# Squared-ReLU MLP of a two-layer encoder trunk: one stream of weight chunks with a fixed order on every engine, and seven instead of five of sixteen row-tile pairs in Strassen's form

## The chip, the cores and the metric

The kernel runs on one NeuronCore of a Trainium2 chip, as one launch. The metric is the device time of one execution in microseconds; lower is better. Inputs and output are float32.

## The reference

The trunk has two layers on a sequence of S = 256 tokens with D = 2048 features. Layer 0 mixes tokens with a convolution module, layer 1 with latent attention; each is followed by the same kind of MLP, with an RMS norm ahead of every part and one at the end.

```python
D_MODEL = 2048; SEQ = 256; DEPTH = 2; D_FF = 4 * D_MODEL

def sq_relu_mlp(h, w1, w2):
    return jnp.square(jax.nn.relu(h @ w1)) @ w2

for layer in range(DEPTH):
    h = rms_norm(x, norm_mixer_g[layer])
    x = x + (conv_module(h, ...) if layer % 2 == 0 else mla(h, ...))
    h = rms_norm(x, norm_mlp_g[layer])
    x = x + sq_relu_mlp(h, mlp_w1[layer], mlp_w2[layer])
return rms_norm(x, final_norm_g)
```

w1 is 2048 x 8192 and w2 is 8192 x 2048 in each layer.

## The kernel before

Every float32 factor is split into a high part (`hi`, rounded to the format of the fast matmul, written by ScalarE, L159 and L389) and the rest (`lo`, a subtraction on VectorE, L160 and L390), and a product is three matmuls: hi with hi, lo with hi, hi with lo (`mm3`, L185 to L187). So each weight is loaded once (1 MB units, three `raw` buffers, issued by SyncE, L149), split once in chunks of 128 x 1024 (six buffers, `WB`), and used by both row tiles of 128 tokens.

The MLP goes through the 8192 hidden features in two halves (`HALVES`). In each half, `up` computes the hidden features in eight groups of four blocks of 128: 16 steps over D, each with a 512-column matmul (L514, the weight's hi part against hi and lo of the input side by side) and a 256-column one (L515) for every block. Two blocks make one pair p of the sixteen (`NPAIR`); its square is taken (L521 to L537) and split (L543, L544). Then `down` goes through the 2048 output columns in two column pairs `n2` of 2 x 512, and for each through the sixteen pairs p. A pair p is a product of a 2 x 2 block matrix (two row tiles by two feature blocks) with another (two feature blocks by two column blocks). A plain pair takes 8 block products, 24 matmuls. Where `seven(p)` holds (p = 0, 3, 6, 9, 12), it takes Strassen's form in Winograd's variant: 7 block products, 21 matmuls. Sums of activation blocks are made in `up` on VectorE and GpSimd (tile W, L525 to L533); sums of weight blocks, four tiles T, in `down` on VectorE (L449, L453, L455), and are then split (L389, L390).

The seven products gather in seven of the eight PSUM banks over all pairs of a column pair; the plain pairs add into three of them and the eighth. Behind the last Strassen pair (p = 12) `early` combines four of the banks (copies L431 and L432 on ScalarE, subtractions L433 and L434 on VectorE, L437 and L438 on GpSimd) and adds them to the residual `xs` (`xs_add`, L555); behind the last pair the other four are added. In the second half `prepare` then transposes blocks of `xs` into the next stage's input (L241, L191, L198) and takes the squares for the next norm (L340). In the last column pair of the last layer the three plain pairs behind p = 12 are kept back and computed output block by output block, so that the final norm (`before` with the gain at L1479, then `finish`) can follow block by block.

The order of the MLP's instructions on each engine is chosen by the scheduler of the programming layer from its own estimate of times. The convolution and the attention are written inside `manual_schedule()`, which keeps the written order on each engine within the block and leaves to the scheduler where the block's instructions fall among those outside it. Attention starts with `u_split` of its first weights (L160 with 128 x 576 tiles).

Of the kernel before, what the change touches and what calls it, by code (L numbers as in the profile page):

```python
# [10 lines left out]
F32 = mybir.dt.float32  # L11
# [7 lines left out]
P = 128  # L19
D = 2048  # L20
# [30 lines left out]
FILL_AT = (5, 15)  # L51
N_WARM = 14
# [24 lines left out]
def trunk_kernel(  # L77
# [306 lines left out]
    def split_part(src, eng):  # L384

        _, nj, cols = src.shape
        hi = wpool.tile([P, nj, cols], F32R, tag="hi", name=nm("hi"), bufs=WB)
        lo = wpool.tile([P, nj, cols], F32R, tag="lo", name=nm("lo"), bufs=WB)
        nc.scalar.activation(hi, src, AF.Copy)  # L389
        eng.tensor_tensor(lo, src, hi.bitcast(F32), op=ALU.subtract)  # L390
        return hi, lo
# [14 lines left out]
    def down(w, k_lo, hs, xs_add, prepare, pre, mp, finish=None, before=None):  # L406

        for n2 in range(NNB // 2):
            na, nb = 2 * n2, 2 * n2 + 1
            banks, seen = {}, set()  # L410
            outs = {(1, nb): "P2", (1, na): "Q3", (0, nb): "P4", (0, na): "Q0"}

# [6 lines left out]
            def plain(p, parts, n, t):  # L419
                for k in range(2):  # L420
                    wh, wl = parts[k]
                    gh, gl = (a[:, k, t * P : (t + 1) * P] for a in hs[p])
                    bs = slice((n - na) * NB, (n - na + 1) * NB)
                    mm(outs[t, n], gh, gl, wh[:, 0, bs], wl[:, 0, bs], p == NPAIR - 1 and k == 1)

            def early():

                s1, s5 = (mp.tile([P, NB], F32, tag="v", name=nm("v"), bufs=2) for _ in range(2))
                uv = mp.tile([P, 2, NB], F32, tag="W", name=nm("W"), bufs=1)
                u, v = uv[:, 0, :], uv[:, 1, :]  # L430
                nc.scalar.activation(s1, banks["P1"], AF.Copy)  # L431
                nc.scalar.activation(s5, banks["Q5"], AF.Copy)  # L432
                nc.vector.tensor_tensor(u, s1, banks["Q6"], op=ALU.subtract)  # L433
                nc.vector.tensor_tensor(v, u, banks["Q7"], op=ALU.subtract)  # L434
                xs_add(nb, s1, 1)
                xs_add(nb, v, 0)
                nc.gpsimd.tensor_tensor(u, s5, u, op=ALU.subtract)  # L437
                nc.gpsimd.tensor_tensor(v, s5, v, op=ALU.subtract)  # L438
                xs_add(na, u, 1)
                xs_add(na, v, 0)  # L440

            last = finish is not None and n2 == NNB // 2 - 1
            kept = []
            for p in range(NPAIR):
                raw = load([rows(w, k_lo + 2 * p, 2, na * NB, 2 * NB)], 2)
                if seven(p):
                    x = raw.rearrange("p j (b n) -> p (j b) n", b=2)
                    tt = mp.tile([P, 4, NB], F32, tag="T", name=nm("T"), bufs=1)
                    nc.vector.tensor_tensor(  # L449
                        tt[:, 0:2, :], x[:, 0:1, :].broadcast_to([P, 2, NB]), x[:, 1:3, :], op=ALU.add  # L450
                    )
                    one = split_part(x[:, 1:2, :], nc.vector)
                    nc.vector.tensor_tensor(tt[:, 2, :], tt[:, 0, :], x[:, 2, :], op=ALU.add)  # L453
                    t13 = split_part(tt[:, 0:2, :], nc.vector)
                    nc.vector.tensor_tensor(tt[:, 3, :], tt[:, 2, :], x[:, 3, :], op=ALU.add)  # L455
                    t24 = split_part(tt[:, 2:4, :], nc.vector)
# [1090 lines left out]
```

## Time and profile before

| | us |
|---|---|
| median of 3 runs | 1974.42 (1972.78 to 1976.09) |
| the profiled execution, its own time | 1974.39 |
| its span, first to last instruction | 1972.6 |
| TensorE busy in it | 1945.4 |
| VectorE, ScalarE, GpSimd busy | 1410.4, 1032.7, 311.0 |

The granted TensorE clock is 0.998 over the span. A line of the profile such as L187 is a line of the kernel above. PE is TensorE, DVE VectorE, ACT ScalarE, POOL GpSimd, SP SyncE. TensorE works through the first MLP's `up` and `down` from 316 to 1008 us, and through the second MLP's from 1269 us to the end.

### The profile page before, as it was taken

The page shows a single profiled execution, that of the slowest core. Times are in us where ns is not written, and L with a number is a line of the kernel's source. Part 1 is how long each engine was busy: PE and PEld are TensorE (multiplying, and loading weights), DVE is VectorE, ACT ScalarE, POOL GpSimd, SP SyncE. Part 2 cuts the span into 40 slices and gives each one's busy share as a digit, 9 for nine tenths or more (in the row PEclk, how much of TensorE's full clock was granted, in tenths as well). Part 3 has the DMA queues.
Part 4 walks back from the last instruction along what each step waited for, and adds up shares of the span by engine and source line. Part 5 has one row for each costly group of instructions (what it writes and reads, how often), then busy time and mean ns, then how long its engine had stood idle before and what let it go on. Part 6 is the DMA issues. An engine that isn't in the chain of part 4 may idle for free.

```text
span 1972.6 us, 28263 instructions
## 1 busy us (share of the span) xinstructions
PE 1945.4 (99%) x10940; PEld 1708.3 (87%) x10940; DVE 1410.4 (71%) x2043; ACT 1032.7 (52%) x1481; POOL 311.0 (16%) x260
## 2 busy tenths in 40 slices
PE   7999999999999999999999999999999999999997
PEld 7999888888888888888899998888888888888886
DVE  5999866666787766678776666566677776667786
ACT  5456655444544444455466665544454444445453
POOL 5999300010000101000001310010100001010000
PEclk9999999999999999999999999999999999999999
DMA  8666456655656665565655445566556676565563
GB/s 241 179 185 186 135 192 186 188 188 168 204 198 203 220 188 188 168 206 195 207 168 179 121 150 178 183 187 188 189 178 200 200 226 188 187 189 199 198 203 117
DMA packets 210502, 367.60 MB, mean 186 GB/s; under 512 B 15416, under 2 KB 89792, under 8 KB 210112
## 3 DMA queue, kind: packets, MB, share of 16 engines
q1 hardware_dynamic: 209344, 363.63, 58.1%
q10 hardware_dynamic: 1024, 2.17, 0.3%
q8 instruction: 85, 1.39, 0.3%
q14 instruction: 49, 0.40, 0.1%
HBM read 363.68 MB, written 2.10 MB: 185 GB/s over the span
## 4 chain that ended last, share of the span: by engine, by line
PE 89%; DVE 8%; ACT 1%; DMA 1%; issue 0%; POOL 0%; POOLq 0%; DVEq 0%; ACTq 0%
PE acc L514 24%; PE acc L187 15%; PE acc L186 15%; PE acc L185 15%; PE acc L515 12%; DVE sum L721 6%; PE acc L620 1%; PE acc L621 1%; PE acc L619 1%; PE acc L241 1%; DVE lo L160 1%; PE sum L669 0%; ACT hi L159 0%; PE acc L1317 0%; DMA xs<-in_x 0%
## 5 line engine op out<-in xcount | busy, mean ns | idle before, releaser
L160 DVE TENSOR_TENSOR lo<-raw,hi 128x1024 fp32r<-128x1024 f32 (+1 forms) x550 | 651.4, 1207 | 367.7 <-ACT hi L159 360.9
L159 ACT ACTIVATE hi<-raw 128x1024 fp32r<-128x1024 f32 (+2 forms) x616 | 622.5, 1040 | 432.4 <-PE acc L514 227.4
L514 PE MATMUL acc<-xt,hi 128*128 128x512 f32 x2048 | 710.5, 390 | 0.0
L515 PE MATMUL acc<-xt,lo 128*128 128x256 f32 x2048 | 578.4, 282 | 0.0
L514 PEld LDWEIGHTS acc<-xt,hi 128*128 128x128 f32 x2048 | 384.4, 188 | 79.7
L515 PEld LDWEIGHTS acc<-xt,lo 128*128 128x128 f32 x2048 | 388.0, 189 | 0.1
L187 PE MATMUL acc<-lo,gh 128*128 128x512 f32 x704 | 274.9, 391 | 2.0 <-DVE lo L160 2.0
L185 PE MATMUL acc<-hi,gh 128*128 128x512 f32 x704 | 274.8, 390 | 0.0
L186 PE MATMUL acc<-hi,gl 128*128 128x512 f32 x704 | 274.7, 390 | 0.0
L389 ACT ACTIVATE hi<-T 128x1024 fp32r<-128x1024 f32 x80 | 84.9, 1062 | 161.9 <-DVE T L449 72.6
L721 DVE SCALAR_TENSOR_TENSOR sum<-ub,w_dw,sum 128x256 f32<-128x256 f32 x400 | 163.7, 503 | 7.1 <-ACT sum L677 6.0
L160 POOL TENSOR_TENSOR lo<-raw,hi 128x1024 fp32r<-128x1024 f32 x66 | 157.5, 2407 | 23.9 <-ACT hi L159 23.9
L529 POOL TENSOR_TENSOR W<-W 128x256 f32<-128x256 f32 x20 | 31.9, 1598 | 819.9 <-DVE W L525 693.9
L185 PE MATMUL acc<-hi,sh 128*128 128x512 f32 x408 | 159.6, 391 | 0.0
L187 PE MATMUL acc<-lo,sh 128*128 128x512 f32 x408 | 159.0, 390 | 0.0
L187 PEld LDWEIGHTS acc<-lo,gh 128*128 128x128 f32 x704 | 132.8, 189 | 30.0 <-DVE lo L160 2.5
L186 PEld LDWEIGHTS acc<-hi,gl 128*128 128x128 f32 x704 | 132.5, 188 | 27.7
L185 PEld LDWEIGHTS acc<-hi,gh 128*128 128x128 f32 x704 | 132.5, 188 | 27.2
L619 PE MATMUL acc<-xt,hi 128*128 128x256 f32 x512 | 144.6, 282 | 0.0
L620 PE MATMUL acc<-xt,hi 128*128 128x256 f32 x512 | 143.2, 280 | 0.5 <-DVE xt L198 0.5
L621 PE MATMUL acc<-xt,lo 128*128 128x256 f32 x512 | 143.2, 280 | 0.3 <-POOL lo L160 0.3
L390 DVE TENSOR_TENSOR lo<-T,hi 128x1024 fp32r<-128x1024 f32 x80 | 97.9, 1225 | 51.6 <-ACT hi L389 51.3
(264 smaller groups left out, 2655.3 us busy)
## 6 DMA issues: line engine op xcount, KB each, us to landing
raw<-in_mlp_w SPq DMA_DIRECT2D x256, 1024.0 KB, 5.5
raw<-in_conv_w_pw SPq DMA_DIRECT2D x64, 512.0 KB, 5.1
raw<-in_conv_w_pw SPq DMA_DIRECT2D x16, 1024.0 KB, 5.0
raw<-in_mla_w_o SPq DMA_DIRECT2D x16, 1024.0 KB, 5.5
raw<-in_mla_w_kv_up SPq DMA_DIRECT2D x8, 1024.0 KB, 5.5
raw<-in_mla_w_in SPq DMA_DIRECT2D x8, 576.0 KB, 3.7
raw<-in_mla_w_in SPq DMA_DIRECT2D x4, 1024.0 KB, 7.1
raw<-in_mla_w_q_up SPq DMA_DIRECT2D x16, 256.0 KB, 3.6
```

Of the source, the lines that this page charges most:

```text
L159: nc.scalar.activation(hi, raw[:, js, :], AF.Copy)
L160: eng.tensor_tensor(lo, raw[:, js, :], hi.bitcast(F32), op=ALU.subtract)
L185: nc.tensor.matmul(ps, sh, mh, start=start, stop=False)
L186: nc.tensor.matmul(ps, sl, mh, start=False, stop=False)
L187: nc.tensor.matmul(ps, sh, ml, start=False, stop=stop)
L390: eng.tensor_tensor(lo, src, hi.bitcast(F32), op=ALU.subtract)
L514: nc.tensor.matmul(ps[b], wh[:, bs], xhl(k), start=k == 0, stop=False)
L515: nc.tensor.matmul(ps[b][:, :S], wl[:, bs], xh(k), start=False, stop=k == KC - 1)
L619: nc.tensor.matmul(o, wh[:, bs], xh(k), start=k == 0, stop=False)
L620: nc.tensor.matmul(o, wh[:, bs], xl(k), start=False, stop=False)
L621: nc.tensor.matmul(o, wl[:, bs], xh(k), start=False, stop=k == KC - 1)
L721: nc.vector.scalar_tensor_tensor(out=out, in0=ubs[c][:, w : w + S], scalar=tap(c, w), in1=pcs[c], op0=ALU.mult, op1=ALU.add)
```

## The change

The MLP is written as a list of units (one weight load each) that consist of chunks; `stream` goes through the chunks of both halves, `up` and `down`, in one loop inside `manual_schedule()`. Ahead of chunk n's matmuls it queues the splits up to chunk n + 5, one chunk at a time, and behind each split at most one piece of other work from a list `todo` (squares, their splits, the steps of `early`, the norm, the transposes). A Strassen pair is four chunks of 3, 6, 6 and 6 matmuls, a plain pair two of 12. The weight sums T need two tiles at a time, not four: the second two overwrite the first two, and their split (`t24`) is put off until behind the next chunk's split.

The Strassen pairs are p = 1, 3, ... 13 in three of the four halves, and p = 0, 2, ... 12 in the last one. `early` is queued in three steps. The two `prepare` steps that stood at the end of the first MLP are run within the first projection of attention, at its steps 4 and 8. The convolution's taps `w_dw` move from the constant pool to the convolution's own pool.

```diff
+SEVENS = ((1, 3, 5, 7, 9, 11, 13),) * 3 + ((0, 2, 4, 6, 8, 10, 12),)
...
-    seven = lambda p: p % 3 == 0 and p < NPAIR - 1
-    LAST_SEVEN = max(p for p in range(NPAIR) if seven(p))
+    N_SEVEN = len(SEVENS[0])
...
+    class Unit:
+        def __init__(self, src, nj, chunks):
+            self.src, self.nj, self.chunks = src, nj, chunks
+
+    class Chunk:
+        def __init__(self, prep, run, after=(), now=None, flush=False):
+            self.prep, self.run, self.after, self.now, self.flush = prep, run, after, now, flush
+
+    def hi_lo(n):
+        return [wpool.tile([P, n, NB], F32R, tag=c, name=nm(c), bufs=WB) for c in ("hi", "lo")]
+
+    def split_into(parts, src):
+        nc.scalar.activation(parts[0], src, AF.Copy)
+        nc.vector.tensor_tensor(parts[1], src, parts[0].bitcast(F32), op=ALU.subtract)
+
+    def stream(units, todo):
+
+        raws, parts, late = {}, {}, []
+
+        def start(u):
+            if u < len(units):
+                raws[u] = load([units[u].src], units[u].nj)
+
+        chunks = [(u, c) for u, unit in enumerate(units) for c in range(len(unit.chunks))]
+        done = [0]
+
+        def prep():
+            n = done[0]
+            if n == len(chunks):
+                return
+            done[0] += 1
+            u, c = chunks[n]
+            held = late[:]
+            late.clear()
+            if units[u].chunks[c].flush:
+                while held:
+                    held.pop(0)()
+            more = units[u].chunks[c].prep(raws[u], parts.setdefault(u, {}))
+            if more is not None:
+                late.append(more)
+            for fn in held:
+                fn()
+            if c == units[u].last_read:
+                start(u + 3)
+
+        for u in range(3):
+            start(u)
+        for n, (u, c) in enumerate(chunks):
+            while done[0] < min(n + WB, len(chunks)):
+                prep()
+                if todo:
+                    todo.pop(0)()
+            if done[0] == len(chunks):
+                while late:
+                    late.pop(0)()
+                for fn in todo[: 2 if n < len(chunks) - 1 else None]:
+                    todo.remove(fn)
+                    fn()
+            chunk = units[u].chunks[c]
+            chunk.run(parts[u])
+            if chunk.now is not None:
+                chunk.now()
+            todo += chunk.after
+        while todo:
+            todo.pop(0)()
...
+        def up_unit(hs, c0, u, ps, after):
+
+            def chunk(h):
+                def prep(raw, parts):
+                    parts[h] = hi_lo(2)
+                    split_into(parts[h], raw[:, 2 * h : 2 * h + 2, :])
+
+                def run(parts):
+                    if not ps:
+                        ps.extend(acc_tile() for _ in range(4))
+                    wh, wl = parts.pop(h)
+                    for j in range(2):
+                        k = 4 * u + 2 * h + j
+                        for b in range(4):
+                            bs = slice(b * P, (b + 1) * P)
+                            nc.tensor.matmul(ps[b], wh[:, j, bs], xhl(k), start=k == 0, stop=False)
+                            nc.tensor.matmul(ps[b][:, :S], wl[:, j, bs], xh(k), start=False, stop=k == KC - 1)
+
+                return Chunk(prep, run, after if h == 1 else [])
+
+            unit = Unit(rows(w1, 4 * u, 4, c0, NB), 4, [chunk(h) for h in range(2)])
+            unit.last_read = 1
+            return unit
...
+        def up_steps(mp, hs, sevens, p, ps, b2):
+
+            held = {}
+
+            def square():
+                v = mp.tile([P, 2, S], F32, tag="v", name=nm("v"), bufs=2)
+                for b in range(2):
+                    nc.scalar.activation(v[:, b, :], ps[2 * b2 + b][:, S:], AF.Copy)
+                for b in range(2):
...
+            def part():
+                hs[p] = held["hl"]
+                split_into(hs[p], held["src"])
+
+            return square, part
...
+
+                def first():
+                    nc.scalar.activation(s1, banks["P1"], AF.Copy)
+                    nc.scalar.activation(s5, banks["Q5"], AF.Copy)
+                    nc.vector.tensor_tensor(u, s1, banks["Q6"], op=ALU.subtract)
+                    nc.vector.tensor_tensor(v, u, banks["Q7"], op=ALU.subtract)
+
+                def second():
+                    xs_add(nb, s1, 1)
+                    xs_add(nb, v, 0)
+                    nc.gpsimd.tensor_tensor(u, s5, u, op=ALU.subtract)
+                    nc.gpsimd.tensor_tensor(v, s5, v, op=ALU.subtract)
+
+                def third():
+                    xs_add(na, u, 1)
+                    xs_add(na, v, 0)
+
+                return [first, second, third]
+
+            def end():
+                for t, n in ((0, nb), (1, nb), (1, na), (0, na)):
+                    xs_add(n, banks[outs[t, n]], t)
+                if last:
+                    pre.extend((prepare, n) for n in (na, nb))
+
+            def finale():
+                before(nssq)
                 for t in range(T):
                     for n in (nb, na):
                         for p, parts in kept:
+                            for k in range(2):
+                                plain(p, k, parts[k], n, t)
                         xs_add(n, banks[outs[t, n]], t)
                         prepare(n, t)
+                    finish(nssq, t)
+
+            def plain_unit(p):
+
+                def chunk(k):
+                    def prep(raw, parts):
+                        parts[k] = hi_lo(2)
+                        split_into(parts[k], raw[:, k, :].rearrange("p (b n) -> p b n", b=2))
+
+                    def run(parts):
+                        if tail and p > last_seven:
+                            if k == 0:
+                                kept.append((p, parts))
+                            if p == NPAIR - 1 and k == 1:
+                                finale()
+                            return
+                        for t in range(T):
+                            for n in (na, nb):
+                                plain(p, k, parts[k], n, t)
+
+                    after = []
+                    if p == NPAIR - 2 and last and n2 == NNB // 2 - 1:
+                        after = [next_prepare]
+                    if k == 1 and p == NPAIR - 1 and not tail:
+                        return Chunk(prep, run, now=end)
+                    return Chunk(prep, run, after)
+
+                return [chunk(k) for k in range(2)], 1
+
+            def seven_unit(p):
+
+                x, tt = [], []
+                gh_gl = lambda f: (a[:, f, :] for a in hs[p])
+
+                def run(names):
+                    def fn(parts):
+                        for name, f, key, i in names:
+                            part = parts[key]
+                            mm(name, *gh_gl(f), part[0][:, i, :], part[1][:, i, :],
+                               p == last_seven and name in ("P1", "Q5", "Q6", "Q7"))
+                    return fn
+
+                def one(raw, parts):
+                    x.append(raw.rearrange("p j (b n) -> p (j b) n", b=2))
+                    tt.append(mp.tile([P, 2, NB], F32, tag="T", name=nm("T"), bufs=1))
+                    parts["one"] = hi_lo(1)
+                    nc.vector.tensor_tensor(
+                        tt[0], x[0][:, 0:1, :].broadcast_to([P, 2, NB]), x[0][:, 1:3, :], op=ALU.add
+                    )
+                    split_into(parts["one"], x[0][:, 1:2, :])
+
+                def two(raw, parts):
+                    parts["two"] = hi_lo(2)
+                    split_into(parts["two"], x[0][:, 2:4, :])
+
+                def t13(raw, parts):
+                    parts["t13"] = hi_lo(2)
+                    split_into(parts["t13"], tt[0])
+                    for i in range(2):
+                        nc.vector.tensor_tensor(tt[0][:, i, :], tt[0][:, 0, :], x[0][:, 2 + i, :], op=ALU.add)
+
+                def t24(raw, parts):
+                    parts["t24"] = hi_lo(2)
+                    return lambda: split_into(parts["t24"], tt[0])
+
+                return [
+                    Chunk(one, run([("P1", A11, "one", 0)]), flush=True),
+                    Chunk(two, run([("Q3", S4, "two", 0), ("P2", A12, "two", 1)])),
+                    Chunk(t13, run([("Q5", S1, "t13", 0), ("Q7", S3, "t13", 1)])),
+                    Chunk(
+                        t24, run([("Q6", S2, "t24", 0), ("P4", A22, "t24", 1)]),
+                        now=todo_early if p == last_seven else None,
+                    ),
+                ], 2
+
+            def todo_early():
+                first, *others = early()
+                first()
+                todo[:0] = others
+
+            made = []
+            for p in range(NPAIR):
+                chunks, last_read = seven_unit(p) if p in sevens else plain_unit(p)
+                unit = Unit(rows(w2, hf * nkh + 2 * p, 2, na * NB, 2 * NB), 2, chunks)
+                unit.last_read = last_read
+                made.append(unit)
+            return made
...
+                        after = []
+                        if u == KC // 4 - 1:
+                            (sa, pa), (sb, pb) = (up_steps(mp, hs, sevens, 2 * g + b2, ps, b2) for b2 in range(2))
+                            after = [sa, sb, pa, pb]
+                            if g == nkh // 4 - 1 and hf == 0:
+                                after.append(norm)
+                            if g == nkh // 4 - 1 and hf == HALVES - 1 and last_w1 is not None:
+                                after.append(last_w1)
+                        units.append(up_unit(hs, (hf * nkh + 4 * g) * P, u, ps, after))
+                for n2 in range(NNB // 2):
+                    units += down_units(mp, hs, sevens, hf, n2)
+
+            with tc.manual_schedule():
+                stream(units, todo)
+            return made_stage[0][0], [lambda fn=fn, n=n: fn(n) for fn, n in pre]
...
-        w_dw = const.tile([P, W * KC], F32, name="w_dw")
+        w_dw = cv.tile([P, W * KC], F32, name="w_dw")
...
-    ssq = mlp(0, ssq, g_mix[1])
+    ssq, due = mlp(0, ssq, g_mix[1])
...
+                if k in (4, 8):
+                    due.pop(0)()
```

More of the change, by code (lines that the diff above doesn't have):

```diff
@@ L417, in mm, with plain @@
                 seen.add(name)
[L419 to L424, printed above, removed]
+            def plain(p, k, part, n, t):
+                gh, gl = (a[:, k, t * P : (t + 1) * P] for a in hs[p])
+                bs = n - na
+                mm(outs[t, n], gh, gl, part[0][:, bs, :], part[1][:, bs, :], p == NPAIR - 1 and k == 1)
             def early():
@@ L477, in down @@
-            if last:
-                before()
+                def first():
[8 more added lines that the diff above has]
+                    nc.gpsimd.tensor_tensor(v, s5, v, op=ALU.subtract)
```

170 lines of the change are left out of this document (45 added, 125 removed).

## The prediction

> **What bounds the kernel now.** I read the page first, then the waits of TensorE, then busy time by stage, then the last 30 us in order of time.
>
> ```profile
> span 1972.6 us, 28263 instructions
> ...
> PE 1945.4 (99%) x10940; PEld 1708.3 (87%) x10940; DVE 1410.4 (71%) x2043; ACT 1032.7 (52%) x1481; POOL 311.0 (16%) x260
> ...
> PE 89%; DVE 8%; ACT 1%; DMA 1%; issue 0%; POOL 0%; POOLq 0%; DVEq 0%; ACTq 0%
> ```
>
> TensorE is busy for 99% of the span, and 89% of the chain that ended last is its own work. A busy TensorE need not be one that never waits, so the next view is the list of what it waited for (these are its second and third rows; the first is the start-up):
>
> ```profile
> PE sum L669 <- DVE ub L644: 2.1, 1, 2.1
> PE acc L187 <- DVE lo L160: 2.0, 1, 2.0
> ```
>
> L669 is in the convolution. The only wait in either MLP is the 2.0 us on a split weight (L160). So in the MLP, time goes where matmuls go. Their price comes from the stretches of the second product (`down`), each of which holds two column pairs of one half; the last row is the end of the program:
>
> ```profile
> 494.40:661.60 167.20, 167.20 (x740) 138.53 (x739) 131.12 (x136) 83.31 (x92) 7.72 (x4) 1.00 0.62 204
> 839.20:1008.30 169.10, 169.10 (x757) 140.22 (x756) 132.56 (x144) 88.37 (x111) 7.84 (x6) 1.00 0.59 195
> 1447.40:1614.70 167.30, 167.30 (x741) 138.60 (x739) 131.16 (x137) 83.42 (x92) 7.72 (x4) 1.00 0.62 204
> 1943.00:1956.00 13.00, 10.96 (x42) 8.56 (x41) 9.01 (x10) 2.25 (x4) 3.86 (x2) 0.87 0.00 0
> ```
>
> Columns: stretch, its length, then busy time of PE, PE weight loads, DVE, ACT and POOL, then clock, DMA share and GB/s. By the code a column pair has 11 plain pairs of row tiles with 24 matmuls and 5 Strassen pairs with 21, which is 369, so a stretch holds 738 (the row counts 740, with two of the neighbours). 167.2 / 738 = 0.2266 us from one matmul to the next, with no gap. A matmul that goes away is worth that, as long as VectorE and ScalarE still deliver the split weights in time. VectorE is the near one: 131 of 167 us. DMA is at 0.62 and is not it.
>
> **Fewer matmuls.** Two more pairs of sixteen take Strassen's form, in 2 column pairs x 2 halves x 2 layers = 8 passes: 16 pairs, each 3 matmuls fewer, 48 in all. 48 x 0.2266 = 10.9 us off the path. [...]
>
> **More work on VectorE.** The groups of VectorE in the first of these stretches:
>
> ```profile
> L160 DVE TENSOR_TENSOR lo<-raw,hi 128x1024 fp32r<-128x1024 f32 x47 | 55.0, 1221 | 20.9 <-ACT hi L159 20.9
> L390 DVE TENSOR_TENSOR lo<-T,hi 128x1024 fp32r<-128x1024 f32 x18 | 22.1, 1226 | 12.2 <-ACT hi L389 12.1
> L390 DVE TENSOR_TENSOR lo<-raw,hi 128x512 fp32r<-128x512 f32 (+1 forms) x18 | 17.2, 953 | 0.0
> L449 DVE TENSOR_TENSOR T<-raw 128x1024 f32<-128x1024 f32 x9 | 11.0, 1223 | 0.0
> L555 DVE SCALAR_TENSOR_TENSOR xs<-W,r,xs 128x512 f32<-128x512 f32 x6 | 6.4, 1090 | 2.4 <-POOL W L438 2.4
> L453 DVE TENSOR_TENSOR T<-T,raw 128x512 f32<-128x512 f32 x9 | 6.2, 688 | 0.0
> L455 DVE TENSOR_TENSOR T<-T,raw 128x512 f32<-128x512 f32 x9 | 6.2, 685 | 0.0
> L555 DVE SCALAR_TENSOR_TENSOR xs<-acc,r,xs 128x512 f32<-128x512 f32 x7 | 5.0, 746 | 0.2 <-PE acc L187 0.2
> ```
>
> A Strassen pair costs VectorE 1.22 + 0.69 + 0.69 for the sums T, 2 x 1.23 for their lo parts and 17.2 / 9 = 1.91 for the other two lo parts: 6.96 us, against 21 x 0.2266 = 4.76 on TensorE. So a Strassen pair by itself is bound by VectorE. A plain pair costs 2 x 1.22 = 2.44 against 5.44. The new lists alternate them: 9.40 us of VectorE against 10.20 of TensorE per two pairs. For a whole half, four more pairs change form, which adds 4 x (6.96 - 2.44) = 18.1: 131.1 + 18.1 = 149.2 us, while TensorE falls to (738 - 12) x 0.2266 = 164.5. That is 91% instead of 78%. On totals it fits, but it has to fit in order too.
>
> **The fixed order, walked once.** Six hi/lo buffers, so the split of a chunk waits until TensorE is through with the chunk six before it; an alternating Strassen and plain pair has just six chunks (3, 6, 6, 6, 12 and 12 matmuls). ScalarE's part of a split:
>
> ```profile
> L389 ACT ACTIVATE hi<-T 128x1024 fp32r<-128x1024 f32 x80 | 84.9, 1062 | 161.9 <-DVE T L449 72.6 <-PE acc L186 45.2 <-DVE T L455 21.7
> ```
>
> Let TensorE start a chunk `one` at 0; its six chunks end at 0.68, 2.04, 3.40, 4.76, 7.48 and 10.20. The next t13: buffer at 3.40, ScalarE to 4.46, lo to 5.69, the two further sums to 7.06. The plain chunk behind it: buffer at 7.48, ScalarE to 8.54, lo to 9.76. Then the t24 that was put off: ScalarE done at 9.6, lo at 10.99. TensorE reaches that t24 at 10.20 + 3.40 = 13.60, so 2.6 us are in hand, and this is the tightest of the six (the second plain chunk is ready at 12.5 and wanted at 17.7; the next `one` at 14.4, wanted at 20.4). In this cover lies the whole cost of the added VectorE work, so I take it at nothing. Without it, each Strassen pair would cost up to 6.96 - 4.76 = 2.2 us, that is 56 x 2.2 = 123 us in the program; that is the upper end, from which the plain pairs between them keep it.
>
> The combination of the products (`early`, `end`) is queued on VectorE in three steps, each between two splits: two subtractions of about 0.69, one add like the 0.75 row, three like the 1.09 row, and 4 x 0.75 at the end, 8.4 us per pass. Behind the last Strassen pair come two or three plain pairs before the next one, each with 5.44 - 2.44 = 3.0 us to spare, so 6 to 9 us plus the 2.6: covered, perhaps short by some tenths where it is two. In `up` nothing gets longer; the squares and their splits are the same instructions, one step behind each split. Loads are issued when the last reader of a unit has been queued, three units ahead as before, in the same 1 MB pieces on the same queue, at a DMA share of 0.62: nothing.
>
> **The tail.** The last 30 us in order of time:
>
> ```profile
> 1939.68 0.58 ACT L431 ACTIVATE v<-acc 128x512 f32<-128x512 f32 x1
> ...
> 1943.18 0.39 PE L185 MATMUL acc<-hi,gh 128*128 128x512 f32 x1
> ...
> 1948.40 0.39 PE L185 MATMUL acc<-hi,gh 128*128 128x512 f32 x1
> 1948.88 0.75 DVE L555 SCALAR_TENSOR_TENSOR xs<-W,r,xs 128x512 f32<-128x512 f32 x1 [1.18 <-POOL W L438]
> 1949.55 2.35 DVE L160 TENSOR_TENSOR lo<-raw,hi 128x1024 fp32r<-128x1024 f32 x2
> 1950.82 0.50 PE L187 MATMUL acc<-lo,gh 128*128 128x512 f32 x1 [2.04 <-DVE lo L160]
> ...
> 1952.88 0.63 PE L185 MATMUL acc<-hi,gh 128*128 128x512 f32 x1
> ...
> 1963.65 0.75 DVE L555 SCALAR_TENSOR_TENSOR xs<-acc,r,xs 128x512 f32<-128x512 f32 x1 [2.17 <-PE acc L187]
> ```
>
> VectorE stood in an add that waited for GpSimd, the last lo parts were queued behind it, and TensorE waited 2.04 us for them. Then its clock fell: 0.87 on average in 1943 to 1956, matmuls of 0.63 us. The three kept pairs are 72 matmuls, 72 x 0.2266 = 16.3, so from 1943.18 they could be through at 1959.5; the add behind the last one began at 1963.65, some 0.2 after it. So 3.9 us are lost here, 2.0 to the wait and 1.9 to the clock. In the new order the last lo part stands ahead of all four adds that read W and v, and only the two subtractions stand before it: with t the end of the last Strassen matmul, ScalarE has the two copies (0.58 each, as L431) by t + 0.9 and the last hi by t + 1.9, VectorE the subtractions by t + 2.3 and the last lo by t + 3.4 to 3.5. TensorE wants it after 5 chunks x 3 x 0.2266 = t + 3.4, and its lo two matmuls later at t + 3.85. Just in time, so I take the wait as gone. Against it stands that the final gain, which the old order had put early,
>
> ```profile
> 1891.59 0.68 DVE L1479 TENSOR_TENSOR xs<-xs,gf 128x512 f32<-128x512 f32 x1
> ```
>
> now comes as four such instructions behind those adds. The four adds last to about t + 8, since two of them wait for GpSimd; the gain lasts to t + 10.7; the first row tile's two adds, squares and finish take, as an estimate, another 5 to 6 us. So VectorE is free for the last adds around t + 16.5, when TensorE ends (t + 16.3): 0 to 0.7 late, taken as 0.4. Tail: 3.9 - 0.4 = 3.5 us won. The ends are 3.9 and, if the last lo is late and the clock falls again, about -1; I take the upper part by the walk. [...]
>
> **The seam to attention.** Two of four `prepare` steps go from the end of the first MLP into the first projection of attention (16 transposes, their evacuations and four squares, with TensorE's share unchanged). It wants each four steps, some 6 us, after it is issued. I take 0; from -0.4 (the seam shortens) to +3 (a late block).
>
> **Sum.** Against its own 1974.39 (span 1972.6 and 1.8 around it; the median of the runs is 1974.42, the same): 1974.4 - 10.9 - 3.5 = 1960.0.
>
> **Rivals.** (1) Part of it is lost: the tail's wait stays, or the t24 margin of 2.6 us is overrun at the start or end of a pass. The tail alone gives 1963.5; 0.5 to 0.8 us in each of 8 passes more gives 1967.5 to 1970. For it: the walk leaves 0.4 us in the tail. (2) The seams are held in written order. If the first splits of a stage queue behind the last adds of the one before, then the MLP-to-attention seam costs 4 x 0.75 + 0.75 = 3.7 and the two seams into an MLP 1.06 + 1.22 = 2.3 each, and each a clock fall of 1.9 as in the tail: 14.0, and the time is 1974. Against it: attention is such a block of fixed order already, and its first splits ran ahead of the MLP's last add:
>
> ```profile
> 1001.02 2.33 DVE L160 TENSOR_TENSOR lo<-raw,hi 128x576 fp32r<-128x576 f32 x3
> ...
> 1008.99 0.74 DVE L555 SCALAR_TENSOR_TENSOR xs<-acc,r,xs 128x512 f32<-128x512 f32 x1
> ```
>
> (3) Slower: VectorE becomes the bound in `down`. In the groups above it stood idle 20.9 + 12.2 = 33.1 us per half, waiting for ScalarE's hi. If those waits belong to the order of the work, a half takes 149.2 + 33.1 = 182.3 instead of 164.5, 17.8 x 4 = 71 us more, and the time is about 2031. It decides from 164.5 - 149.2 = 15.3 us of such waits per half. Against it: ScalarE itself was held by TensorE there, which is a producer that ran ahead:
>
> ```profile
> ACT hi L159 <- issue: 23.4, 8, 3.4
> ACT hi L389 <- DVE T L449: 19.3, 9, 4.6
> ACT hi L389 <- PE acc L186: 15.6, 7, 3.4
> ACT hi L159 <- PE acc L186: 10.2, 3, 3.4
> ```
>
> and the walk, whose waits all end on TensorE's buffers. That the change does not do what it says is no case: the lists of seven are in the code, and the matmul count follows.
>
> **How the numbers follow.** Forecast 1957 to 1963: 0.70. Rival 1, 1963 to 1970: 0.13. Better than 1957 (smoother seams): 0.03. Rival 2: 0.07. Rival 3, from some 1980 on: 0.07. 0.2% is 3.9 us, about what a measurement of this kernel can tell from no change; faster by more means below 1970.5, which the first three cases are: 0.86; same 0.07; slower 0.07. The range 1956 to 1970 holds the forecast and rival 1.
>
> **What would show it.** Right: 48 matmuls fewer in all; a half of `down` near 164.5 us; VectorE there at 145 to 150; no wait of TensorE at the end and a clock of 1.00 until the last matmul. Wrong: TensorE waiting for lo at t24 in most passes (rivals 1 and 3), or once for 2 to 4 us at 317, 1000 or 1260 us (rival 2); `down` longer than 167 us would refute the whole sum.

## The result, and the profile after

The changed kernel takes 1968.84 us (median of 6 runs, 1965.46 to 1969.05), the kernel before 1974.37 in the same session (6 runs, 1972.78 to 1976.09): ratio 0.9968, 95% interval [0.9955, 0.9981]. It is faster by 5.5 us; 14.4 were forecast. The profiled execution took 1969.05, of which 1966.9 are its span. From the page:

```profile
span 1966.9 us, 28422 instructions
...
PE 1939.8 (99%) x10892; PEld 1695.0 (86%) x10892; DVE 1521.8 (77%) x2123; ACT 1070.4 (54%) x1511; POOL 334.8 (17%) x284
...
PE 94%; DVE 2%; ACT 1%; DMA 1%; issue 1%; POOL 0%; POOLq 0%; DVEq 0%; ACTq 0%; SPq 0%
```

The 48 matmuls are gone (10940 to 10892), and 94% of the chain that ended last is now TensorE's own work. The longest waits of TensorE, without the start-up:

```profile
PE acc L186 <- DVE v L506: 1.5, 1, 1.5
PE sum L823 <- DVE ub L798: 1.1, 1, 1.1
PE acc L1462 <- DVE pr L1456: 1.1, 2, 0.9
```

The wait for a split weight at the end is gone; a new wait of 1.5 us, on L506 (a square of `up`), has come. Busy time by stage: the convolution's first product, then `up` and `down` of the four halves in turn (columns as in the prediction):

```profile
20.00:200.00 180.00, 180.00 (x1523) 179.82 (x1522) 168.04 (x426) 103.71 (x173) 168.83 (x107) 1.00 0.68 188
318.65:500.16 181.51, 181.51 (x1032) 157.73 (x1031) 122.46 (x155) 88.94 (x119) 19.95 (x21) 1.00 0.59 182
500.16:664.86 164.70, 164.70 (x729) 136.42 (x727) 152.82 (x165) 94.48 (x103) 8.68 (x4) 1.00 0.64 204
664.86:842.24 177.38, 177.38 (x1025) 155.87 (x1023) 118.95 (x127) 86.15 (x108) 20.00 (x21) 1.00 0.61 190
842.24:1008.78 166.54, 166.54 (x745) 138.08 (x743) 152.21 (x168) 97.47 (x118) 7.92 (x6) 1.00 0.61 192
1270.21:1448.33 178.12, 178.12 (x1031) 156.62 (x1031) 117.82 (x127) 88.47 (x116) 20.22 (x21) 1.00 0.60 186
1448.33:1613.04 164.71, 164.71 (x728) 136.38 (x727) 152.88 (x165) 94.61 (x104) 8.68 (x4) 1.00 0.64 205
1613.04:1790.42 177.38, 177.38 (x1024) 155.87 (x1023) 117.34 (x128) 85.21 (x106) 17.73 (x21) 1.00 0.61 189
1790.42:1956.98 166.56, 165.03 (x727) 136.08 (x726) 150.85 (x168) 94.17 (x112) 8.21 (x4) 1.00 0.58 184
```

The same stretches of the kernel before that matter most, the convolution and the first `up`:

```profile
20.00:200.00 180.00, 180.00 (x1544) 179.82 (x1543) 168.70 (x427) 106.28 (x179) 170.20 (x108) 1.00 0.64 188
...
316.10:494.24 178.14, 178.14 (x1032) 158.16 (x1031) 116.67 (x165) 90.98 (x122) 14.09 (x15) 1.00 0.58 183
```

`down` went as forecast: 164.7 us where no seam lies in the stretch (164.5 forecast, 167.4 before in the same boundaries). But in 180 us of convolution TensorE got through 1523 matmuls instead of 1544, and the first `up` took 181.51 instead of 178.14, both busy without a gap and at a clock of 1.00. The change adds no work to either. The groups of TensorE in the first `up`, before:

```profile
L514 PE MATMUL acc<-xt,hi 128*128 128x512 f32 x512 | 177.7, 391 | 0.0
L515 PE MATMUL acc<-xt,lo 128*128 128x256 f32 x512 | 144.6, 282 | 0.0
```

and after:

```profile
L488 PE MATMUL acc<-xt,hi 128*128 128x512 f32 x512 | 181.1, 397 | 0.0
L489 PE MATMUL acc<-xt,lo 128*128 128x256 f32 x512 | 144.2, 282 | 0.0
```

The same 512 instructions on the same shapes last 397 ns instead of 391; the 3.4 us between 177.7 and 181.1 are the 3.37 by which the stage is longer.

Spans, stage by stage (start of the stage to start of the next; `down` 2 with attention, because the two moved `prepare` steps cross that border):

| stage | before | after | difference |
|---|---|---|---|
| start to first `up` | 316.10 | 318.65 | +2.55 |
| `up` 1 | 178.14 | 181.51 | +3.37 |
| `down` 1 | 167.41 | 164.70 | -2.71 |
| `down` 2 and attention | 430.11 | 427.97 | -2.14 |
| `down` 3 | 167.41 | 164.71 | -2.70 |
| `down` 4 to the last matmul | 171.13 | 166.56 | -4.57 |
| last matmul to the end | 9.36 | 9.93 | +0.57 |
| `up` 2, 3 and 4 | 532.91 | 532.88 | -0.03 |

The sum is -5.66. With 12 matmuls x 0.2266 = 2.72 in each of the four `down`, it falls into -10.88 for the matmuls, +5.92 for the slower convolution and first `up`, +0.58 at the seam to attention, +1.49 for the new wait, and -2.77 in the tail (-4.57 + 2.72 - 1.49 + 0.57). The +2.55 is itself a balance: 21 matmuls of 118 ns are 2.5, the wait at the start-up is 0.6 longer (12.2 instead of 11.6), that on `xt` 0.5 longer, and that on `ub` 1.0 shorter (1.1 instead of 2.1).

### The profile page after: what moved, and what is told of

Its sections match the earlier page's. It is cut to its first block, busy times and chain, and to the rows that moved or that the text cites. A ratio compares the mean times of both kernels' runs of the same rounds, so it can differ in the third digit from the quotient of the medians.

```text
span 1966.9 us, 28422 instructions
## 1 busy us (share of the span) xinstructions
PE 1939.8 (99%) x10892; PEld 1695.0 (86%) x10892; DVE 1521.8 (77%) x2123; ACT 1070.4 (54%) x1511; POOL 334.8 (17%) x284
## 4 chain that ended last, share of the span: by engine, by line
PE 94%; DVE 2%; ACT 1%; DMA 1%; issue 1%; POOL 0%; POOLq 0%; DVEq 0%; ACTq 0%; SPq 0%
PE acc L488 24%; PE acc L186 15%; PE acc L187 15%; PE acc L188 15%; PE acc L489 12%; PE acc L775 3%; PE acc L774 3%; PE acc L773 3%; PE acc L242 1%; PE sum L823 0%; DVE lo L413 0%; PE acc L1471 0%; DMA xs<-in_x 0%; DMA raw<-in_mlp_w 0%; PE acc L1335 0%
## 5 line engine op out<-in xcount | busy, mean ns | idle before, releaser
L413 DVE TENSOR_TENSOR lo<-raw,hi 128x1024 fp32r<-128x1024 f32 (+1 forms) x512 | 610.6, 1203 | 282.0 <-ACT hi L412 279.6
L412 ACT ACTIVATE hi<-raw 128x1024 fp32r<-128x1024 f32 (+1 forms) x512 | 512.9, 1012 | 480.4 <-PE acc L488 317.4
L186 PE MATMUL acc<-hi,gh 128*128 128x512 f32 x576 | 224.3, 389 | 0.0
L188 PE MATMUL acc<-lo,gh 128*128 128x512 f32 x576 | 224.1, 389 | 0.0
L187 PE MATMUL acc<-hi,gl 128*128 128x512 f32 x576 | 224.1, 389 | 0.0
L186 PE MATMUL acc<-hi,sh 128*128 128x512 f32 x520 | 203.5, 391 | 1.5 <-DVE v L506 1.5
L160 ACT ACTIVATE hi<-raw 128x1024 fp32r<-128x1024 f32 (+2 forms) x184 | 179.9, 1005 | 42.2 <-PE acc L187 38.2
L188 PE MATMUL acc<-lo,sh 128*128 128x512 f32 x520 | 202.8, 390 | 0.0
L161 DVE TENSOR_TENSOR lo<-raw,hi 128x1024 fp32r<-128x1024 f32 (+2 forms) x118 | 133.2, 1147 | 65.1 <-ACT hi L160 59.5
L187 PE MATMUL acc<-hi,sl 128*128 128x512 f32 x392 | 152.5, 389 | 0.0
```

The costliest lines, as they stand in the source:

```text
L160: nc.scalar.activation(hi, raw[:, js, :], AF.Copy)
L161: eng.tensor_tensor(lo, raw[:, js, :], hi.bitcast(F32), op=ALU.subtract)
L186: nc.tensor.matmul(ps, sh, mh, start=start, stop=False)
L187: nc.tensor.matmul(ps, sl, mh, start=False, stop=False)
L188: nc.tensor.matmul(ps, sh, ml, start=False, stop=stop)
L412: nc.scalar.activation(parts[0], src, AF.Copy)
```

## The experiments

In the tables of the layout (bytes within a partition), `hi` begins at 47872 before and at 45888 after, 1984 lower; `lo`, `raw`, `xs` and the small tiles move by the same. 1984 bytes is the size of `w_dw`, which left the constant pool. `xt`, the input of the convolution and of `up`, stays at 196384, and the convolution's own tiles stay too (its `xn` at 101376). That gave the first theory: the place of the buffers makes the matmuls slower, not the order.

**The changed kernel again**, with no edit.

> The changed kernel once more, nothing edited. It came 9 us short of the forecast; 5.9 of them are two stretches in which TensorE ran the same matmuls at a longer spacing though its clock was 1.00 and it waited for nothing: the convolution (11.59 us per channel block instead of 11.43) and the first product of the first MLP's first half (181.5 us instead of 178.1). Theory A (where the buffers lie: the hi, lo and raw buffers moved by 1984 bytes, so that they start at 64 instead of 0 modulo 128): the same two stretches are slow in the profile again, and the times lie at 1965 to 1969. Theory B (a state that a run falls into by chance): in the profile one or both of the stretches may be at the old spacing, and the times fall into groups that differ by 3.4 (one stretch) and 2.5 us (the other).

1968.95 us (8 runs, 1968.92 to 1969.44), ratio 0.9974 [0.9963, 0.9984]. Every stage of its trace repeats to 0.05 us but for the start (318.51). Both slow stretches are there again (1523 matmuls in the 180 us of convolution). One thing doesn't fit a layout that is always slow: two of the six runs of the result took 1965.46 and 1965.68, some 3.4 us less than the other four, and that is what the first `up` has in excess (their mean clock, 0.999, is no higher than that of most of the slower four). No trace of them is kept, so whether this place is slow in every execution stays open.

**The kernel before, with only `w_dw` moved.**

```diff
-        w_dw = const.tile([P, W * KC], F32, name="w_dw")
+        w_dw = cv.tile([P, W * KC], F32, name="w_dw")
```

> The kernel before with one line of the change alone: w_dw moves to the convolution's own pool, which moves hi, lo and raw by 1984 bytes to 64 modulo 128; order and matmuls are the old ones. Theory A (place of the buffers): the convolution at 11.59 us per block and the first product of the first half at 181.5, so 2 to 6 us slower than before: 1976 to 1980. Theory B (chance): like before, 1974.4, the stretches at 11.43 and 178.1 as often as in the kernel before. Rival C (the fixed order or the longer program causes it): like before, 1974.4.

1979.35 us (7 runs, 1977.54 to 1981.04), ratio 1.0027 [1.0017, 1.0038]. Its convolution and first `up`:

```profile
20.00:200.00 180.00, 180.00 (x1523) 179.81 (x1522) 168.03 (x426) 103.76 (x173) 168.89 (x107) 1.00 0.69 188
...
318.66:500.17 181.51, 181.51 (x1032) 157.73 (x1031) 117.29 (x165) 91.05 (x122) 14.15 (x15) 1.00 0.57 179
```

The same 1523 and the same 181.51: this line alone makes both stretches slow, without the rest of the change.

**The kernel before, the buffers 64 bytes higher**, `w_dw` in its old pool: is it the tile or the place? (The second pad comes on top of the first for the convolution's own tiles, which lie 128 bytes higher, `xn` at 101504.)

```diff
-PAD_CONST = 24
+PAD_CONST = 40
...
+        cv.tile([P, 16], F32, name="pad_cv")
```

> The kernel before with nothing but 64 bytes more of padding at the start of the constants (and 64 in the convolution's pool, so that its other tiles keep their place modulo 128): hi, lo and raw start at 64 modulo 128. Theory A (the place of hi, lo and raw modulo 128 sets the spacing): as with w_dw moved, the convolution 2.5 us longer and the first product of the first half 181.5 us, 1979 to 1981. Rival D (it was the move of w_dw, whose columns VectorE and ScalarE read as scalars, and not the buffers): like before, 1974.4.

1980.66 us (6 runs, 1977.37 to 1980.76), ratio 1.0028 [1.0016, 1.0041].

```profile
20.00:200.00 180.00, 180.00 (x1523) 179.82 (x1523) 168.04 (x426) 103.93 (x173) 169.19 (x107) 1.00 0.69 188
320.32:501.83 181.51, 181.51 (x1032) 157.74 (x1032) 117.29 (x165) 91.03 (x122) 14.13 (x15) 1.00 0.57 179
...
1949.40:1962.40 13.00, 10.96 (x49) 8.69 (x48) 10.59 (x12) 3.83 (x6) 3.86 (x2) 1.00 0.00 0
```

A shift by 64 bytes does it, with every instruction unchanged and `w_dw` in its old pool. One of the six runs took 1977.37, again 3.3 less than the slowest four. (Its first `up` starts later still, at 320.32, since here the convolution's second product is slower too: 418 matmuls from 225 to 316 us, where the kernel before has 424.) The last row is the tail: the wait for the last lo parts is there as before,

```profile
1958.81 0.50 PE L187 MATMUL acc<-lo,gh 128*128 128x512 f32 x1 [2.04 <-DVE lo L160]
```

but the clock stays at 1.00 behind it, where the kernel before had 0.87.

**The changed kernel on a multiple of 128 bytes.** Before, `hi` began at a multiple of 128 (47872); after, 64 beside one. The same edit of the two pads in the changed kernel puts it at 45952, a multiple again, and the convolution's own tiles 128 bytes higher.

> The changed kernel with 64 bytes more of padding ahead of the buffers, and 64 bytes in the convolution's pool so that its other tiles keep their place modulo 128: hi, lo and raw start at 0 modulo 128 again. Theory A: both stretches are fast again (11.43 and 178.1), 1968.8 - 5.9 = 1963. Theory B and rival C: no difference, 1965 to 1969.

1964.57 us (5 runs, 1964.41 to 1964.59), ratio 0.9950 [0.9938, 0.9963].

```profile
20.00:200.00 180.00, 180.00 (x1526) 179.82 (x1526) 168.34 (x427) 104.61 (x175) 169.45 (x107) 1.00 0.68 189
...
317.73:495.87 178.14, 178.14 (x1032) 156.85 (x1032) 122.96 (x155) 88.96 (x119) 21.32 (x21) 1.00 0.59 186
```

Half an answer: the first `up` is back at 178.14, but the convolution stays slow (1526).

**The changed kernel at exactly 2048 bytes below the old place**, `PAD_CONST = 8` and the same `pad_cv`: `hi` at 45824. The convolution's own tiles are back at 101376. If the old place modulo 2048 is good, both stretches must come back.

> The changed kernel with the buffers moved so that hi, lo and raw lie exactly 2048 bytes below their place in the kernel before, and the convolution's tiles where they were. With 64 bytes of padding the first product came back to 178.1 us, but the convolution only from 318.5 to 317.7 us, against 316.1 before. Theory A1 (the place modulo 128 is all that counts): like with 64 bytes, 1964.6. Theory A2 (the place modulo 2048, or against the other tiles, counts as well): the convolution ends at 316.1 to 316.7 and the time is 1963.0 to 1963.6.

1962.77 us (5 runs, 1962.71 to 1964.39), ratio 0.9945 [0.9933, 0.9957].

```profile
20.00:200.00 180.00, 180.00 (x1544) 179.82 (x1544) 168.65 (x427) 105.98 (x178) 169.89 (x108) 1.00 0.65 190
316.13:494.26 178.13, 178.13 (x1031) 157.96 (x1031) 123.22 (x155) 89.00 (x119) 20.19 (x21) 1.00 0.59 186
```

1544 matmuls, and `up` starts at 316.13 as before the change (316.10). Some 6 us of the missing gain come back from moving buffers alone, with the change otherwise whole. For the convolution two things changed between the last two kernels, the place of the weight buffers and that of its own tiles; no run separates them.

**The new wait: where a half begins with a Strassen pair.** The last half has the list 0, 2, 4 and so on. Its first pair needs seven PSUM banks, and four of the eight still hold the last sums of `up`. After, VectorE and TensorE at that point:

```profile
1791.78 1.23 DVE L413 TENSOR_TENSOR lo<-raw,hi 128x1024 fp32r<-128x1024 f32 x1 [1.55 <-ACT hi L412]
1792.92 0.75 DVE L506 TENSOR_TENSOR v<-acc,v 128x256 f32<-128x256 f32 x2
1793.71 0.69 DVE L520 SCALAR_TENSOR_TENSOR v<-v 128x512 f32<-128x512 f32 x1
1794.32 1.22 DVE L649 TENSOR_TENSOR T<-raw 128x1024 f32<-128x1024 f32 x1
1795.45 0.68 DVE L413 TENSOR_TENSOR lo<-raw,hi 128x512 fp32r<-128x512 f32 x1
1796.05 0.75 DVE L506 TENSOR_TENSOR v<-acc,v 128x256 f32<-128x256 f32 x2
```

```profile
1796.62 0.47 PE L186 MATMUL acc<-hi,sh 128*128 128x512 f32 x1 [1.50 <-DVE v L506]
```

The second pair of squares (1796.05) frees the banks and stands behind the splits. The other halves begin with a plain pair and have no such wait. First try, in the changed kernel: the last half begins with pair 1.

```diff
-SEVENS = ((1, 3, 5, 7, 9, 11, 13),) * 3 + ((0, 2, 4, 6, 8, 10, 12),)
+SEVENS = ((1, 3, 5, 7, 9, 11, 13),) * 3 + ((1, 3, 5, 7, 9, 11, 12),)
```

> The changed kernel with the last half's list changed from 0, 2, ... 12 to 1, 3, 5, 7, 9, 11, 12, so that its first pair is a plain one (four banks wanted at once, not seven) and the last Strassen pair stays 12. If the 1.5 us wait of TensorE at 1796 us is a wait for PSUM banks that the last squares of the first product still hold, it goes, and the time falls by 1.5 to 1.7 us to about 1967.2. If the two Strassen pairs in a row (11 and 12) overrun VectorE, a wait of 1 to 3 us comes at the end instead, and nothing is won.

1970.08 us (8 runs, 1967.68 to 1972.45), ratio 0.9977 [0.9967, 0.9987]: nothing won.

```profile
PE acc L188 <- DVE lo L413: 1.6, 2, 1.1
```

The bank wait is gone, and waits for lo parts of 1.6 us in all have come at 1943 and 1945 us. By the prediction's prices two Strassen pairs in a row ask 13.92 us of VectorE in 9.52 of TensorE, here right ahead of the end.

Second try, on the kernel with the buffers in the good place: `(1, 3, 5, 7, 8, 10, 12)`.

> The kernel of after_2048 with the last half's list 1, 3, 5, 7, 8, 10, 12: its first pair is plain, as in after_bank, and the two Strassen pairs in a row are 7 and 8, in the middle, with a plain pair ahead of the last one. If the wait at the start of that half was for PSUM banks and the wait that after_bank got at the end was VectorE behind after two Strassen pairs in a row, both are gone: 1.5 us below after_2048. If two in a row cost a wait wherever they stand, 1 to 2 us come back in each column pair and it is like after_2048 or slower.

1963.16 us (5 runs, 1961.92 to 1963.72), ratio 0.9943 [0.9931, 0.9956]; `down` 4 takes 165.61 instead of 166.57. The bank wait is gone; a wait of 0.8 us for a lo part at 1939 remains of VectorE's lag. The median does not show the gain. In the profiled execution the clock fell once, at the end of the convolution's first product:

```profile
206.00:209.40 3.40, 3.40 (x8) 2.77 (x9) 3.40 (x10) 3.40 (x6) 3.32 (x4) 0.51 0.02 5
```

which cost it 1.8 us; in after_2048 the same stretch has 17 matmuls and 1.00. The last section sets the step of the clock ahead of this fall beside the one of after_2048.

Third try, the two neighbouring pairs early: `(1, 3, 4, 6, 8, 10, 12)`.

> The changed kernel with hi, lo and raw 2048 bytes below their place in the kernel before, as in after_2048, and in the last half the Strassen pairs 1, 3, 4, 6, 8, 10, 12: it begins with a plain pair, and the two Strassen pairs that stand side by side (3 and 4) lie eight pairs ahead of the kept ones, not two as in after_mid. Theory (the bank wait comes from a first pair in Strassen's form, VectorE's lag from two such pairs in a row, and it is worked off within a few alternating pairs): no wait of TensorE on a bank at the start of the last half, none on a lo part in the last 30 us; the last down near 164.7 us instead of 166.6 (after_2048) and 165.6 (after_mid), and a time near 1961. Rival (the lag isn't worked off by alternating pairs, which leave VectorE only 0.8 us each): a wait for lo of about 1 us stays, somewhere from pair 4 to the end, and the time stays near 1962 to 1963.

1963.15 us (5 runs, 1961.58 to 1963.36), ratio 0.9943 [0.9929, 0.9956].

```profile
206.00:209.40 3.40, 3.40 (x9) 2.74 (x10) 3.40 (x10) 3.40 (x6) 3.32 (x4) 0.52 0.03 5
...
1785.92:1951.23 165.31, 164.78 (x727) 136.05 (x726) 151.94 (x170) 92.58 (x111) 8.21 (x4) 1.00 0.56 185
```

Neither the bank wait nor a wait in the last 30 us is left; TensorE waits 0.53 once, at 1811, right behind the two neighbours. So the lag is worked off, as the theory had it, and `down` 4 takes 165.31 instead of 166.57 (164.7 was expected). The time of 1961 came in one run of five; the profiled one had the clock fall again, and its 1961.1 us of span less 1.8 would be 1959.3. By medians the three versions at the good place are not to be told apart; their fastest runs, 1962.71, 1961.92 and 1961.58, lie in the order of their last `down` (166.57, 165.61, 165.31).

**The order alone**: after_2048 with the old lists, five Strassen pairs a half.

```diff
-SEVENS = ((1, 3, 5, 7, 9, 11, 13),) * 3 + ((0, 2, 4, 6, 8, 10, 12),)
+SEVENS = ((0, 3, 6, 9, 12),) * 4
```

> The kernel of after_2048 (fixed order, everything at its place) with the old lists, pairs 0, 3, 6, 9 and 12 in every half: the order of the change without its two further Strassen pairs. By the forecast's sum it is 10.9 us slower than after_2048 (48 matmuls of 0.2266 us), about 1974, and a half of the second product takes 167.4 us again instead of 164.7; what the fixed order wins against the kernel before is the 3 us at the end only. If instead the fixed order costs TensorE something in each pass that the fewer matmuls pay for, it is more than 10.9 slower.

1978.56 us (11 runs, 1976.86 to 1979.19), ratio 1.0020 [1.0011, 1.0028].

```profile
PE acc L186 <- DVE v L506: 3.6, 4, 0.9
```

```profile
494.50:663.40 168.90, 167.95 (x740) 138.48 (x739) 136.60 (x144) 89.01 (x97) 8.68 (x4) 1.00 0.61 203
```

A half of `down` takes 168.90, 1.49 more than before (167.41), with a wait on banks in each of the four (the row counts 0.9 of each as waiting, the rest is counted as busy): the fixed order with the old lists is slower than the scheduler's. About 1974 was expected. Its span is 1975.2 us, that of after_2048 1960.6; of the 14.6 between them the 48 matmuls are 10.9, and the three halves that begin with a Strassen pair here and not there are some 4 more. So the new lists win twice here, by fewer matmuls and by beginning with a plain pair.

## Why the prediction was wrong in size

It forecast 1960.0, 1956 to 1970; measured were 1968.84. The sign was right and the main mechanism too; 8.9 us of the 14.4 did not come. That the time lies in the range of rival 1 (1963 to 1970) is luck: neither of its two causes, a wait left in the tail or an overrun t24, is in the trace.

**Fewer matmuls, 10.9: right.** 2.71 and 2.70 us in the two stretches that can be read by themselves, where 12 x 0.2266 = 2.72 were forecast.

**VectorE, nothing: right.** The groups of VectorE in the first `down` after:

```profile
L413 DVE TENSOR_TENSOR lo<-raw,hi 128x1024 fp32r<-128x1024 f32 x52 | 62.9, 1218 | 9.4 <-ACT hi L412 9.3
L413 DVE TENSOR_TENSOR lo<-T,hi 128x1024 fp32r<-128x1024 f32 x27 | 33.0, 1222 | 0.9 <-ACT hi L412 0.3
L662 DVE TENSOR_TENSOR T<-T,raw 128x512 f32<-128x512 f32 x28 | 19.4, 692 | 1.0
L649 DVE TENSOR_TENSOR T<-raw 128x1024 f32<-128x1024 f32 x13 | 15.8, 1217 | 0.0
```

The idle time ahead of the lo parts fell from 33.1 us to 10.3, as it must if those waits came from a producer that ran ahead, and TensorE waited for no lo in any `down`. VectorE is busy for 152.8 instead of the 149.2 forecast and outside the 145 to 150 that were to show it: the stretch now also holds eight small instructions of the norm (1.3 us) and, at its edges, a split and two sums of a further pair (2.6). Rival 3 fell with this, and rival 1 by its mechanism. That after_bank and after_mid ran into waits as soon as two Strassen pairs stood side by side shows that the alternation does carry it.

**"In `up` nothing gets longer": wrong, and the step that failed.** The move of `w_dw` stood in the change and got no price in the sum. It moved the weight buffers by 1984 bytes, and with that the convolution took 2.55 and the first `up` 3.37 us longer: 5.9 of the missing 8.9. Shown by before_wdw and before_pad64 (the place alone makes the kernel before slow) and after_2048 (the place alone makes the changed kernel fast); why a place is slow stays open. No row of the trace of before could price it; what it could have shown was that TensorE in those stages stood at 100% busy, so that any change of a matmul's spacing there goes into the time in full. A bound of a percent or two of the convolution and `up` on both sides would have been honest.

**A wait that was not foreseen, 1.5.** The walk followed hi/lo buffers and not PSUM banks. The last list's pair 0 needs banks that `up` still holds.

**The tail, 3.5: mis-sized.** 2.77 between the two profiles. The walk itself held: the first kept matmul, right behind the last Strassen one, starts at 1940.9 (t), the last lo was forecast for t + 3.4 to 3.5, and in the tail of after it ends at 1944.4:

```profile
1940.90 0.39 PE L186 MATMUL acc<-hi,gh 128*128 128x512 f32 x1
```

```profile
1943.19 1.22 DVE L413 TENSOR_TENSOR lo<-raw,hi 128x1024 fp32r<-128x1024 f32 x1
...
1951.01 1.28 DVE L1635 TENSOR_TENSOR xs<-xs,gf 128x512 f32<-128x512 f32 x2
...
1955.88 1.42 DVE L1657 SCALAR_TENSOR_TENSOR xs<-xs,ys,gf 128x512 f32<-128x512 f32 x2
1957.21 1.41 DVE L545 SCALAR_TENSOR_TENSOR xs<-acc,r,xs 128x512 f32<-128x512 f32 x2
```

The gain lasts to t + 11.4 (10.7 forecast), and VectorE is free at t + 16.4 (16.5 forecast). Two last adds now run one behind the other at TensorE's end (1957.21 to 1958.62), where before only one was left; that is most of the +0.57, where 0.4 was taken. The larger fault is the 1.9 for the clock, which this pair of profiles hides. before_pad64 has the same wait of 2.04 us with no fall behind it, and its last `down` takes 169.61 us where before_wdw takes 171.18 (and before, with the fall, 171.13). So the wait alone does not bring the fall, and a removed wait wins those 1.6 us only in the executions that have one. These traces show the same gap with both outcomes: 2.04 us was followed by a fall in before (0.87 from 1943 to 1956 us) and by none in before_pad64 (1.00 from 1949.4 to 1962.4), so the prediction's one trace does not give the price. The last section shows where the wait lies in the steps of the clock.

**The seam, 0: nearly right**, +0.58 in a range of -0.4 to +3. Rival 2 fell: TensorE waits for no split at 1000 us.

The remaining 0.3 us is in what lies around the span (1.8 before, 2.1 after). Together: 5.9 + 1.5 + 0.7 + 0.6 + 0.3 = 9.0, the difference of the two profiled executions from the forecast.

## What to carry to other kernels

Every line of a diff gets a price, also one that only moves a buffer: where an engine is busy for 100% of a stage, a stretch that is as busy as before with fewer instructions in the same time (here 1523 matmuls instead of 1544 in 180 us) says that each instruction became longer, and a pad of 64 bytes tells the place from the code. When an order is fixed by hand, walk every resource that a stage takes over from the one before it, banks as well as buffers. And a clock fall in one profiled execution is not a cost that an edit wins back in each (here it followed a wait of 2.04 us in before and not in before_pad64): look how the idle time lies in the steps of the clock, and whether the fall follows the wait in a second trace.

## What was not expected of the hardware

With the same instructions, the same order, no waits and a clock of 1.00, TensorE's spacing depended on where the buffers lie: 1523 instead of 1544 matmuls in 180 us of convolution (118.2 ns instead of 116.6), and 397 instead of 391 ns for a 512-column matmul in the first `up`. 64 bytes up or 1984 down made both slow: 1523 matmuls in all five traces with such a place, and 181.51 us for the first `up` in after, before_wdw and before_pad64. 1920 down mended `up` alone (178.14 us, with 1526 matmuls in the convolution), 2048 down both (178.13 us and 1544). `hi`, `lo`, `raw`, `xs` and the small tiles moved together, so which of them counts isn't shown. `up` 2, 3 and 4 use the same buffers and take 177.4 to 178.1 us each in before and in after (532.91 and 532.88 together). Why only the first one is touched, whether the place counts by itself or against `xt`, which never moved, and what the runs at 1965.5 and 1977.4 had that the others had not, stays open; no run separates these. The difference is 1.4% in the convolution and 1.9% in the first `up`. No run shows whether it is TensorE's reads that get slower.

The clock changed at whole steps of 3.413 us. In the clock record of before, full clock from 16.27 to 1951.63 us is 567 such steps, half clock to 1955.04 one, and full clock to 1968.70 four; in that of after, full clock from 15.32 to 1960.92 is 570; both then have a stretch at half clock that the end cuts off. Between these first and last times, a step at half clock, or the start of that last stretch, came in both traces behind each step in which TensorE was busy, as the profile counts it, for 1.37 us or less; behind 1.58 or more it never came. So where a wait lies in the steps may be what gives it two outcomes; no run tests that by itself. These are the steps that hold most of the wait on lo at the end, in before (a fall followed) and before_pad64 (none), and of the wait of 2.0 to 2.1 us on `ub`, in after_mid (a fall) and after_2048 (none):

```profile
1948.22:1951.63 3.41, 1.37 (x7) 0.82 (x6) 2.75 (x3) 0.00 (x0) 0.63 (x1) 1.00 0.00 0
1955.12:1958.53 3.41, 1.64 (x8) 1.03 (x6) 2.23 (x3) 0.00 (x0) 1.71 (x1) 1.00 0.00 0
202.52:205.93 3.41, 1.35 (x12) 1.15 (x11) 3.41 (x11) 1.44 (x3) 2.44 (x4) 1.00 0.73 283
202.08:205.49 3.41, 1.66 (x15) 1.45 (x13) 3.41 (x11) 1.42 (x2) 2.42 (x5) 1.00 0.79 293
```

If it is so, a wait of 2.04 us has to lie almost whole within one step. For steps that lie at random that is, as an estimate from these figures, 4 to 5 executions in 10 (its start has 1.37 us of room in 3.41 if the whole wait has to lie inside, and up to 1.8 if 1.83 us of it do), so the price of the fall in the tail was about 0.7 us on average and not 1.9.

The 48 times of the kernel before beside these runs lie in three groups, 14 at 1972.8 to 1972.9, 29 at 1974.3 to 1974.7 and 5 at 1975.9 to 1976.3. It has two such waits, at 204 and at 1949 us, and a fall costs 1.6 to 1.8 us; that these are runs with none, one and two falls is a reading that fits the one profile, which has one fall and is of the middle group. Of the other groups no trace is kept.
